# RWKV-7 preparation in a two-layer hybrid backbone: key norms inverted per token, products moved between engines, one tile of inverses per layer

## The chip, the cores and the metric

The kernel runs on one core of one Trainium2 chip. The metric is the device time of one execution in microseconds (us); lower is better. The core has a matrix engine (TensorE, PE in the tables; its weight loads are PEld), a vector engine (VectorE, DVE), a scalar engine (ScalarE, ACT), a general engine (GpSimd, POOL) and a queue that issues transfers (SyncE, SP). Each engine takes its instructions in a fixed order, and semaphores hold it where an input or a buffer is not yet ready.

## What is computed

The reference is a backbone of two layers over 256 latent and 256 context tokens of width 1024. In each layer one input projection feeds four token mixers (bidirectional RWKV-7, Hyena, a short gated convolution, grouped-query attention); their outputs are merged by sigmoid gates and projected, and a grouped top-2 mixture of 16 experts follows. The change concerns the RWKV mixer alone, of which this is the core:

```python
def rwkv_inputs(p, mu, w0, w_up, a0, a_up, k_k, k_a):
    ...
    kk = to_heads(k * k_k)
    kk = kk * lax.rsqrt(jnp.maximum(jnp.sum(kk * kk, -1, keepdims=True), 1e-24))
    k_dir = k[None] * (1.0 + (a - 1.0) * k_a)
    return to_heads(r), to_heads(k_dir), to_heads(v), kk, to_heads(a), to_heads(decay), gd

def wkv_scan(S0, r, decay, k, v, kk, a, reverse, emit):
    def step(S, inp):
        r_t, w_t, k_t, v_t, kk_t, a_t = inp
        S = (S * w_t[:, :, None, :]
             - jnp.einsum('bhvk,bhk->bhv', S, kk_t)[..., None] * (kk_t * a_t)[:, :, None, :]
             + v_t[..., :, None] * k_t[..., None, :])
        return S, (jnp.einsum('bhvk,bhk->bhv', S, r_t) if emit else None)
    ...
```

The four heads are 64 channels wide. A key is divided by its own norm, so only the product of the normalised key with itself times the rate a is needed (the kernel uses the square of the norm and one reciprocal). The state is carried from the context tokens to the latent tokens, in both directions; in layer 1 no context output is wanted, so the context stream there computes states only (emit is false).

## The kernel before

Channels lie on the 128 partitions (two heads each), tokens on the free axis. Per layer the program runs attention, then the RWKV input projections, then Hyena and the short convolution, then the RWKV core `recur()`, `merge()` with the gates, the output projection, a layer norm, the router and the experts. That is the order in which the code is written; a list scheduler in the framework sets, from this order as priority and a cost model of its own, one fixed sequence of instructions for each engine. So the many 128x512 projections (`mm3`, three products of split operands on L355 to L357, their weights split by ACT on L326 and by DVE on L327) and the modulation products (L394) stand between the RWKV instructions on PE and fill it there.

`recur()` makes four pairs per layer: stream s (0 context, 1 latent) by half b of the channels. Each pair is a generator `rwkv_pair` with four stages, and `recur()` interleaves them: stages 1 and 2 of the first pair; then, for each pair i, stage 1 of pair i+1, stage 3 of pair i, stage 2 of pair i+1, stage 4 of pair i.

- Stage 1, preparation, in tile R4. `kkr` = k times k_k (ACT, L872) and the squares in `at` (ACT, L873); PE adds the squares of a head with a matrix of ones, which leaves each sum on all 64 rows of its head (L876, 64x256); DVE takes the maximum with 1e-24 (L877), the reciprocal (L878) and the product with `kkr` (L879), giving `kkd`. Then for each direction d: two products on PE (L883, L884), two tanh on ACT (L885, L886, the second into `at` again), a running sum of the log decays on DVE (L889), two small offsets (L891, L892), exponentials on ACT (L894, L895), the directional key `kd` (ACT L896, POOL L898), and the four scaled operands: `ar` (DVE L904, POOL L906 if emit), `be` (DVE L908, L909) and `ka` (POOL L911), and three columns `sc` (L915 to L917). With emit, POOL L923 and DVE L924 prepare the bonus term.
- Stage 2, the triangular inverse. Products on PE (L936), masking on DVE (L938), the bonus on PE (L943, 128x2), a DVE copy (L944). The tile TZ takes the inverses of 16-token-group blocks: POOL clears it (L954, 128x2048) for each pair, DVE runs a serial loop of 15 steps (L968, L970, L976), ACT (L981, four instructions) and DVE (L982) write the result into TZ. TZ's buffer is single, so L954 waits for the last reader of the pair before, in its stage 4. In layer 0 the scratch of stage 2 is tile R4 too, the one of stage 1.
- Stage 3, the inverse level by level: PE L990, ACT L992, PE L998 and L1000, DVE L1003; then PE L1008, ACT L1010, and the second half of the tile (FZ) filled by DVE copies (L1012, L1013, 64x256), PE products and ACT copies (L1019, L1020).
- Stage 4, the recurrence over two groups of 128 tokens and both directions: PE L1039 to L1044 and DVE L1046; PE L1050 and ACT L1052 (`kb`); a scaled state Ss (DVE L1057); PE L1061 and L1064, ACT L1066 (Rs), PE L1070, DVE L1072 (Wn), and with Wn the state update on PE (L1079, L1080), a scaled state Sf (DVE L1077), the sum on DVE (L1099, L1101) and the outputs (PE L1084 to L1089, ACT L1092, DVE L1094).

After `recur()`, `finish()` normalises Y for `merge()`, which handles the branches in the order 2, 3, 1, 0; RWKV is branch 0.

## Time and profile before

| | us |
|---|---|
| median of 3 runs | 1911.12 |
| lowest and highest | 1905.01, 1916.12 |
| the profiled execution | 1914.72 |
| its span, first to last instruction | 1912.9 |
| mean granted clock of TensorE over the span | 0.934 |

| engine | busy, us | share of the span | instructions |
|---|---|---|---|
| PE | 1679.5 | 88% | 9683 |
| PEld | 1109.7 | 58% | 9683 |
| DVE | 884.5 | 46% | 1920 |
| ACT | 530.6 | 28% | 935 |
| POOL | 223.4 | 12% | 263 |

The durations below come from the profiled execution, whose time is 3.6 us above the median; 1.8 us of its time lie outside the span. Its RWKV cores lie at 270 to 510 us (layer 0) and 1250 to 1520 us (layer 1). [...]

### The profile page before, as it was taken

Reading aid. Unit: us, or ns where it says so; the run is one execution under the profiler, and the core shown is the slowest. Engines: PE = TensorE matmul, PEld = TensorE weight load, DVE = VectorE, ACT = ScalarE, POOL = GpSimd, SP = SyncE. Lnnn points to the kernel's source line nnn. Section 1 sums busy time; section 2 is a strip of 40 time slices with the busy share of each in tenths; the row PEclk is TensorE's granted clock in tenths of the full one; section 3 lists DMA queues with packets and bytes.
Section 4 is the critical chain, followed back from the end, with each engine's and each line's share of the span. In section 5 each row is a group of like instructions: output and inputs, shape, how many; then the busy total and the mean of one; then the engine's idle time right before and its main releaser. Section 6 shows DMA issues by size and latency. Waiting matters only on the chain. (4 is left out here: it accounts for less than half of the span.)

```text
span 1912.9 us, 24847 instructions
## 1 busy us (share of the span) xinstructions
PE 1679.5 (88%) x9683; PEld 1109.7 (58%) x9683; DVE 884.5 (46%) x1920; ACT 530.6 (28%) x935; POOL 223.4 (12%) x263
## 2 busy tenths in 40 slices
PE   4799999999999987999999919989889996999982
PEld 1467666766778875444444306767778895444430
DVE  4364458778554565101010076585887676200003
ACT  2253233433223311111011044543443352111101
POOL 4200121011000031000000041021120002000001
PEclk7899999999999995999999959988899997999996
DMA  9513553111243255883979953265212357879994
GB/s 367 212 40 131 183 188 111 50 62 51 76 138 116 101 196 191 287 337 117 378 273 375 403 196 129 82 224 192 67 62 86 117 180 289 337 281 420 420 421 163
DMA packets 123350, 384.82 MB, mean 201 GB/s; under 512 B 8791, under 2 KB 75103, under 8 KB 92383
## 3 DMA queue, kind: packets, MB, share of 16 engines
q1 hardware_dynamic: 106176, 329.41, 46.0%
q10 hardware_dynamic: 10238, 33.23, 4.7%
q0 software_dynamic: 6816, 20.58, 3.0%
q8 instruction: 77, 1.26, 0.3%
q14 instruction: 43, 0.34, 0.1%
HBM read 361.62 MB, written 21.56 MB: 200 GB/s over the span
## 5 line engine op out<-in xcount | busy, mean ns | idle before, releaser
L357 PE MATMUL acc<-hB,cv 128*128 128x512 f32 (+1 forms) x864 | 309.4, 359 | 9.9 <-POOL hB L616 9.8
L355 PE MATMUL acc<-hA,cv 128*128 128x512 f32 (+1 forms) x864 | 309.2, 358 | 7.1 <-ACT hA L610 3.9
L356 PE MATMUL acc<-hA,cv 128*128 128x512 f32 (+1 forms) x864 | 308.1, 357 | 4.2 <-DVE cv L327 4.2
L355 PEld LDWEIGHTS acc<-hA,cv 128*128 128x128 f32 x864 | 166.2, 192 | 44.6 <-issue 10.1
L357 PEld LDWEIGHTS acc<-hB,cv 128*128 128x128 f32 x864 | 165.8, 192 | 44.5 <-issue 12.8
L356 PEld LDWEIGHTS acc<-hA,cv 128*128 128x128 f32 x864 | 166.1, 192 | 34.4 <-issue 8.4
L327 DVE TENSOR_TENSOR cv<-ring,cv 128x1024 fp32r<-128x1024 f32 (+1 forms) x108 | 128.6, 1197 | 41.9 <-ACT cv L326 39.6
L1415 DVE TENSOR_TENSOR y<-XS,k 128x512 f32<-128x512 f32 x15 | 15.4, 1029 | 266.4 <-PE k L1403 265.7
L326 ACT ACTIVATE cv<-ring 128x1024 fp32r<-128x1024 f32 (+1 forms) x108 | 109.1, 1019 | 27.7 <-DMA ring<-in_w_in_dram 22.4
L1403 PE MATMUL k<-R,R 128*64 128x512 f32 (+1 forms) x288 | 108.5, 600 | 2.9 <-DMA R<-in_exp_w_dram 2.9
L394 PE MATMUL ada<-ring,csf 128*32 128x512 f32 x336 | 63.4, 665 | 13.3 <-ACT csf L230 10.1
L1403 PEld LDWEIGHTS k<-R,R 128*64 128x64 f32 (+1 forms) x288 | 36.6, 152 | 56.5 <-issue 50.8
L1323 ACT ACTIVATE gt<-acc 128x512 f32<-128x512 f32 (+1 forms) x64 | 31.3, 488 | 110.9 <-PE acc L357 102.7
L1403 PE MATMUL acc<-R,R 128*64 128x512 f32 (+1 forms) x160 | 60.3, 594 | 1.7 <-DMA R<-in_exp_w_dram 1.7
L1415 DVE TENSOR_TENSOR y<-XS,acc 128x512 f32<-128x512 f32 x7 | 7.2, 1028 | 114.4 <-PE acc L1403 114.4
L1332 DVE SCALAR_TENSOR_TENSOR gt<-gt,o 128x512 f32<-128x512 f32 (+1 forms) x48 | 26.5, 552 | 69.6 <-PE o L357 66.1
L1403 PE MATMUL k<-ring,R 128*64 128x512 f32 (+1 forms) x144 | 54.4, 609 | 0.0
L968 DVE TENSOR_TENSOR R<-R 128x32 f32<-128x32 f32 (+14 forms) x120 | 50.9, 424 | 1.7
L1535 DVE CAST m_ix<-o 128x1 int32<-128x1 f32 x14 | 2.2, 159 | 106.2 <-PE o L1533 106.2
L355 PE MATMUL o<-R,R 128*128 128x512 f32 (+1 forms) x128 | 45.7, 358 | 2.9 <-DVE R L1330 2.9
L357 PE MATMUL o<-R,R 128*128 128x512 f32 (+1 forms) x128 | 45.6, 358 | 1.1 <-DVE R L327 1.1
L1435 PE MATMUL k<-R,y 128*64 128x512 f32 (+1 forms) x124 | 45.6, 593 | 0.8 <-DVE y L1420 0.8
(565 smaller groups left out, 3386.7 us busy)
## 6 DMA issues: line engine op xcount, KB each, us to landing
R<-in_exp_w_dram SPq DMA_DIRECT2D x87, 1024.0 KB
ring<-in_w_in_dram SPq DMA_DIRECT2D x51, 1024.0 KB
ring<-in_ada_w_dram SPq DMA_DIRECT2D x42, 1024.0 KB
ring<-in_exp_w_dram SPq DMA_DIRECT2D x34, 1024.0 KB
cv<-in_exp_w_dram SPq DMA_DIRECT2D x31, 1024.0 KB
hB<-in_exp_w_dram SPq DMA_DIRECT2D x24, 1024.0 KB
TZ<-in_exp_w_dram SPq DMA_DIRECT2D x16, 1024.0 KB
y<-in_w_branch_dram SPq DMA_DIRECT2D x32, 256.0 KB
```

The costliest lines, as they stand in the source:

```text
L326: first = ACT.activation(hi, src, AF.Copy)
L327: DVE.tensor_tensor(lo, src, hi.bitcast(F32), op=OP.subtract)
L355: PE.matmul(o, lh, rh, start=start, stop=False)
L356: PE.matmul(o, ll, rh, start=False, stop=False)
L357: PE.matmul(o, lh, rl, start=False, stop=stop)
L394: PE.matmul(po[32 * q:32 * q + 32, :], csf[:, 2 * k:2 * k + 32], t[:, 512 * q:512 * q + 512], start=(k == 0), stop=(k == 7), skip_group_ch ...
L968: DVE.tensor_tensor(P4[:, :, :, :i + 1], T4[:, :, :, :i + 1], row[:, None, :, :].to_broadcast([128, 8, 2, i + 1]), op=OP.mult)
L1323: ACT.activation(gt, gp, AF.Tanh, scale=0.5)
L1332: DVE.scalar_tensor_tensor(gt, gt, 1.0, q, op0=OP.add, op1=OP.mult)
L1403: PE.matmul(q[c, :], t[:, k, c], w[x](k), start=(k == 0), stop=(k == 7), skip_group_check=n > 1)
L1415: DVE.tensor_tensor(t.rearrange("p (k c) -> p c k", k=4), act.rearrange("p (c k) -> p c k", k=4), p3.rearrange("p (c k) -> p c k", k=4), o ...
L1435: PE.matmul(p[h][c, :], t[:, k, c], w2[x](k)[:, h * 512:h * 512 + 512], start=(k == 0), stop=(k == 3), skip_group_check=n > 1)
```

## The change

It touches `recur()` and `rwkv_pair` in four ways.

- The key norms are inverted per token. The squares are now the stationary operand and `hones` (128x2, ones in the rows of one head per column) the moving one, so that PE leaves the four sums of a token on its own row (tokens on partitions, 128x4; new line L880). DVE takes maximum and reciprocal of the 128x4 tile `kkn` (L882, L883). ACT spreads the result, times -0.5, over 64 columns per head into `at` (L885), PE transposes the two 128x128 halves (L888), and DVE multiplies `kkr` with the product in PSUM (L889).
- The products on POOL (L898, L906, L911 and L923 of before: 16, 12, 16 and 6 instructions in a run) are DVE's (L908, L916, L921, L933).
- Four kinds of DVE instruction are ACT's: the FZ copies (L1012, L1013, 16 each), Ss (8), Wn (32) and Sf (16).
- The tile TZ is taken once per layer, in `recur()`, and cleared there as a whole. The pairs after the first clear the 1024 columns of the TZ half alone (new L964); FZ's zero blocks stay from the first clearing. The clearing now waits for the readers of the TZ half, in stage 3 of the pair before, and no more for those of FZ in its stage 4.

```diff
--- before.py
+++ after.py
@@ -798,8 +798,12 @@
         def recur():
             N8 = wt("y0", [128, 1024]).rearrange("p (m t) -> p m t", m=8)
             POOL.tensor_copy(N8, ident[:, None, :].to_broadcast([128, 8, 128]))
-
-            pairs = [rwkv_pair(l, s, b, ctx_out or s == 1, kT[b], rT[b], V, Y, wad, wa, bon, N8)
+            tz = unit("TZ")
+            TZ = tz[:, :1024].rearrange("p (m x t) -> p m x t", m=8, x=2)
+            FZ = tz[:, 1024:].rearrange("p (m t) -> p m t", m=8)
+            POOL.memset(tz, 0.0)
+
+            pairs = [rwkv_pair(l, s, b, ctx_out or s == 1, kT[b], rT[b], V, Y, wad, wa, bon, N8, TZ, FZ)
                      for s in range(2) for b in range(2)]
             next(pairs[0])
             next(pairs[0])
@@ -850,7 +854,7 @@
 
         return recur, finish
 
-    def rwkv_pair(l, s, b, emit, kTb, rTb, V, Y, wad, wa, bon, N8):
+    def rwkv_pair(l, s, b, emit, kTb, rTb, V, Y, wad, wa, bon, N8, TZ, FZ):
 
         ts_ = slice(256 * s, 256 * s + 256)
         k_, r_ = kTb[:, ts_], rTb[:, ts_]
@@ -872,11 +876,17 @@
         ACT.activation(kkr, k_, AF.Copy, scale=col("rwkv_k_k", l, b))
         ACT.activation(at, k_, AF.Square, scale=col("rwkv_k_k", l, b))
         q = rps()
-        for hp in heads:
-            PE.matmul(q[hp, :256], cc("ones")[hp, :64], at[hp, :], start=True, stop=True)
-        DVE.tensor_scalar(kkd, q[:, :256], 1e-24, None, op0=OP.max)
-        DVE.reciprocal(kkd, kkd)
-        DVE.scalar_tensor_tensor(kkd, kkd, -0.5, kkr, op0=OP.mult, op1=OP.mult)
+        for g in range(2):
+            PE.matmul(q[:, 2 * g:2 * g + 2], at[:, g * 128:g * 128 + 128], cc("hones"), start=True, stop=True)
+        n2 = wt("kkn", [128, 4])
+        DVE.tensor_scalar(n2, q[:, :4], 1e-24, None, op0=OP.max)
+        DVE.reciprocal(n2, n2)
+        n64 = at.rearrange("p (g h c) -> p (g h) c", g=2, h=2)
+        ACT.activation(n64, n2[:, :, None].to_broadcast([128, 4, 64]), AF.Copy, scale=-0.5)
+        q = rps()
+        for g in range(2):
+            PE.transpose(q[:, g * 128:g * 128 + 128], at[:, g * 128:g * 128 + 128], ident)
+        DVE.tensor_tensor(kkd, kkr, q[:, :256], op=OP.mult)
         AR, BE, KA, SC = [], [], [], []
         for d in range(2):
             q, qa = rps(), rps()
@@ -895,7 +905,7 @@
                 ACT.activation(en3[:, g], cu[:, g], AF.Exp, scale=0.5 * KAPPA, bias=mb[:, 1, g:g + 1])
             ACT.activation(kd[d], at, AF.Identity, scale=col("rwkv_k_a", l, b, pd),
                            bias=pf[:, l * 2 + b:l * 2 + b + 1])
-            POOL.tensor_tensor(kd[d], kd[d], k_, op=OP.mult)
+            DVE.tensor_tensor(kd[d], kd[d], k_, op=OP.mult)
             if d == 0:
                 inc, prev, inv = ep3[:, :, 1:], ep3[:, :, :128], en3[:, :, 1:]
             else:
@@ -903,12 +913,12 @@
             ar = E(512).rearrange("p (g x t) -> p g x t", g=2, x=2)
             DVE.tensor_tensor(ar[:, :, 0, :], g2(kkr), prev, op=OP.mult)
             if emit:
-                POOL.tensor_tensor(ar[:, :, 1, :], g2(r_), inc, op=OP.mult)
+                DVE.tensor_tensor(ar[:, :, 1, :], g2(r_), inc, op=OP.mult)
             be = E(256)
             DVE.scalar_tensor_tensor(be, at, 1.0, kkd, op0=OP.add, op1=OP.mult)
             DVE.tensor_tensor(g2(be), g2(be), inv, op=OP.mult)
             ka = E(256)
-            POOL.tensor_tensor(g2(ka), g2(kd[d]), inv, op=OP.mult)
+            DVE.tensor_tensor(g2(ka), g2(kd[d]), inv, op=OP.mult)
 
             sc = wt("ssc", [128, 3], bufs=4)
             e_in, e_out = (en3[:, :, 0:1], ep3[:, :, 128:129]) if d == 0 else (ep3[:, :, 128:129], en3[:, :, 0:1])
@@ -920,7 +930,7 @@
             KA.append(ka)
             SC.append(sc)
         if emit:
-            POOL.tensor_tensor(kd[0], kd[0], kd[1], op=OP.add)
+            DVE.tensor_tensor(kd[0], kd[0], kd[1], op=OP.add)
             DVE.scalar_tensor_tensor(kd[0], r_, col("rwkv_r_k", l, b), kd[0], op0=OP.mult, op1=OP.mult)
         yield
 
@@ -950,10 +960,8 @@
         ad = G_(256).rearrange("p (s u) -> p s u", u=8)
         TT_ = G_(256).rearrange("p (c j) -> p c j", c=8)
         o2 = G_(256).rearrange("p (c k u) -> p c k u", c=8, k=4)
-        tz = unit("TZ")
-        POOL.memset(tz, 0.0)
-        TZ = tz[:, :1024].rearrange("p (m x t) -> p m x t", m=8, x=2)
-        FZ = tz[:, 1024:].rearrange("p (m t) -> p m t", m=8)
+        if s or b:
+            POOL.memset(TZ.rearrange("p m x t -> p (m x t)"), 0.0)
         POOL.tensor_copy(TT_.rearrange("p c j -> p (c j)"), msk[:, 1024:1280])
         for x in range(4):
             xs_ = slice(32 * x, 32 * x + 32)
@@ -1009,8 +1017,8 @@
         xs = wt("XS", [128, 8, 64])
         ACT.activation(xs[lo_], q[lo_].rearrange("p (m t) -> p m t", m=8), AF.Copy)
         for hp in heads:
-            DVE.tensor_copy(FZ[hp, 0:4, hp], TZ[hp, 0:4, 1, :])
-            DVE.tensor_copy(FZ[hp, 4:8, hp], TZ[hp, 4:8, 0, :])
+            ACT.activation(FZ[hp, 0:4, hp], TZ[hp, 0:4, 1, :], AF.Copy)
+            ACT.activation(FZ[hp, 4:8, hp], TZ[hp, 4:8, 0, :], AF.Copy)
         q = rps()
         for m in range(4):
             PE.matmul(q[lo_, m * 64:m * 64 + 64], TZ[lo_, m, 0, :], xs[lo_, m, :], start=True, stop=True)
@@ -1054,7 +1062,7 @@
                 S = SBD[d, b]
                 if not first and step == 0:
                     Ss = wt("Ss", [128, 128], bufs=2)
-                    DVE.tensor_scalar(Ss, S, sc[:, 0:1], None, op0=OP.mult)
+                    ACT.activation(Ss, S, AF.Copy, scale=sc[:, 0:1])
                     S = Ss
                 q = rps()
                 for h in range(2):
@@ -1069,12 +1077,12 @@
                     hv = slice(h * 64, h * 64 + 64)
                     PE.matmul(q[:, hv], FZ[:, 4 * d + 2 * g + h, :], R[:, hv], start=True, stop=True)
                 W = wt("Wn", [128, 128], bufs=2)
-                DVE.tensor_copy(W, q[:, :128])
+                ACT.activation(W, q[:, :128], AF.Copy)
                 if update:
                     f = sc[:, 1 + step:2 + step]
                     if not first:
                         Sf = wt("Sf", [128, 128], bufs=2)
-                        DVE.tensor_scalar(Sf, S, f, None, op0=OP.mult)
+                        ACT.activation(Sf, S, AF.Copy, scale=f)
                     q = rps()
                     PE.matmul(q[:, :128], kb[:, 0, :], Vg, start=True, stop=False)
                     PE.matmul(q[:, :128], kb[:, 1, :], W, start=False, stop=True)
```

The sequences change as follows in three places. The names are tiles with their buffer numbers: k_ and acc_ are PSUM, R_ the working tiles, cst the constants (ones, `hones`, the identity), kkn_ the new 128x4 tile, cv_ and ring_ the weights of the projections.

PE, layer 0, preparation of the first pair, before:

```order
L357 MATMUL acc_1691<-hB_50_303,cv_229_1688 128x512
L876 MATMUL k_1727<-R_233_1724,cst 64x256 x2
L883 MATMUL k_1733<-R_146_866 128x256
L884 MATMUL k_1734<-R_146_866 128x256
L883 MATMUL k_1759<-R_146_866 128x256
L884 MATMUL k_1760<-R_146_866 128x256
```

and after:

```order
L357 MATMUL acc_1691<-hB_50_303,cv_229_1688 128x512
L880 MATMUL k_1729<-cst,R_234_1726 128x2 x2
L394 MATMUL ada_3359<-ring_3357,csf 32x512 x4
L355 MATMUL acc_3370<-hA_47_300,cv_513_3367 128x512
L356 MATMUL acc_3370<-hA_47_300,cv_513_3367 128x512
L357 MATMUL acc_3370<-hB_49_302,cv_513_3367 128x512
L355 MATMUL acc_3370<-hA_47_300,cv_513_3367 128x512
L356 MATMUL acc_3370<-hA_47_300,cv_513_3367 128x512
L888 MATMUL k_1736<-cst,R_234_1726 128x128 x2
L893 MATMUL k_1740<-R_146_866 128x256
L894 MATMUL k_1741<-R_146_866 128x256
```

Four modulation products and five projection products now stand between the norm's products and the transposes, and the products for the tanh (L893, L894) come behind the transposes.

PE, layer 1, preparation of the first pair, before:

```order
L356 MATMUL acc_7866<-hA_1140_6964,cv_1275_7863 128x256
L357 MATMUL acc_7866<-hB_1142_6966,cv_1275_7863 128x256
L876 MATMUL k_8340<-R_1324_8337,cst 64x256 x2
L883 MATMUL k_8346<-R_1243_7538 128x256
L884 MATMUL k_8347<-R_1243_7538 128x256
```

and after:

```order
L356 MATMUL acc_7883<-hA_1145_6981,cv_1280_7880 128x256
L357 MATMUL acc_7883<-hB_1147_6983,cv_1280_7880 128x256
L880 MATMUL k_8359<-cst,R_1330_8356 128x2 x2
L888 MATMUL k_8366<-cst,R_1330_8356 128x128 x2
L893 MATMUL k_8370<-R_1248_7555 128x256
L894 MATMUL k_8371<-R_1248_7555 128x256
```

Here the transposes stand directly behind the norm's products. In the other pairs of layer 1 there are about 100, 11 and 22 rows between the two; in the third and fourth of layer 0 there are five projection products, in the second three modulation and seven projection products.

ACT, layer 0, preparation of the second pair, before:

```order
L981 ACTIVATE TZ_1804<-R_246_1803 32x8x32 x4
L872 ACTIVATE R_249_1852<-R_144_864,pc 128x256
L873 ACTIVATE R_249_1852<-R_144_864,pc 128x256
L1323 ACTIVATE gt_3503<-acc_3478 128x512
L326 ACTIVATE cv_532_3562<-ring_3513 128x1024
L885 ACTIVATE R_249_1852<-k_1861,pd 128x256
L886 ACTIVATE R_249_1852<-k_1862,pd 128x256
```

and after:

```order
L1331 ACTIVATE gt_3520<-acc_3495 128x512
L876 ACTIVATE R_251_1857<-R_144_864,pc 128x256
L877 ACTIVATE R_251_1857<-R_144_864,pc 128x256
L326 ACTIVATE cv_537_3579<-ring_3530 128x1024
L326 ACTIVATE R_507_3350<-y_509_3354 128x512
L885 ACTIVATE R_251_1857<-kkn_1863 128x256
L895 ACTIVATE R_251_1857<-k_1871,pd 128x256
L896 ACTIVATE R_251_1857<-k_1872,pd 128x256
```

The spreading of the inverses (L885) stands behind two splits of weights (L326), and the tanh behind it.

## Rows read from the trace of the kernel before

**Rows 1.** Stretches: columns are us, busy (x) per engine, PEclk, DMA share, GB/s.
```profile
270.00:510.00 240.00, 221.45 (x1888) 163.69 (x1886) 187.49 (x451) 92.06 (x182) 37.41 (x41) 0.96 0.23 80
510.00:700.00 190.00, 189.15 (x857) 152.50 (x857) 94.86 (x157) 55.91 (x77) 16.94 (x12) 1.00 0.34 111
1250.00:1520.00 270.00, 245.71 (x2308) 206.51 (x2306) 204.75 (x501) 109.33 (x216) 43.14 (x47) 0.92 0.34 112
310.00:320.00 10.00, 6.85 (x46) 4.06 (x47) 6.42 (x13) 6.91 (x14) 0.72 (x1) 0.67 0.00 0
```

**Rows 2.** Waits of PE, 250 to 550 us: total, times, longest.
```profile
PE k L990 <- DVE TZ L1003: 6.3, 4, 2.7
PE k L876 <- ACT R L873: 5.2, 3, 3.4
PE k L936 <- DVE R L909: 2.0, 1, 2.0
...
PE k L883 <- DVE R L877: 1.0, 1, 1.0
```

**Rows 3.** Waits of PE, 1230 to 1640 us.
```profile
PE k L990 <- DVE TZ L982: 6.3, 5, 2.4
...
PE acc L356 <- DVE cv L327: 3.7, 2, 2.8
PE o L355 <- DVE R L1330: 2.9, 2, 1.9
PE o L1135 <- DVE R L1132: 2.2, 1, 2.2
```

**Rows 4.** Timeline of PE, layer 0: start, us, instruction, idle before.
```profile
271.09 0.65 PE L876 MATMUL k<-R,cst 64*64 64x256 f32 x4
...
287.05 0.58 PE L943 MATMUL k<-cst,R 128*128 128x2 f32 x4 [0.44 <-DVE R L924]
...
313.15 0.91 PE L876 MATMUL k<-R,cst 64*64 64x256 f32 x4 [3.35 <-ACT R L873]
```

**Rows 5.** One line of PE: ns min/median/max, first and last start.
```profile
L1050 PE MATMUL k<-cst,R x24: 271/273/273, 340.4 to 1491.2; 128*128 128x128 f32 x24
```

**Rows 6.** Groups of DVE by form: busy, mean ns | idle before, releaser.
```profile
L878 DVE RECIPROCAL R<-R 128x256 f32<-128x256 f32 x8 | 14.0, 1747 | 0.1
...
L1072 DVE COPY Wn<-k 128x128 f32<-128x128 f32 x32 | 9.3, 290 | 20.7 <-PE k L1070 20.6
...
L1012 DVE COPY TZ<-TZ 64x256 f32<-64x256 f32 x16 | 4.6, 285 | 0.3
L879 DVE SCALAR_TENSOR_TENSOR R<-R 128x256 f32<-128x256 f32 x8 | 4.3, 537 | 0.0
L1269 DVE RECIPROCAL amx<-amx 128x1 f32<-128x1 f32 x24 | 3.9, 162 | 4.4 <-ACT R L1268 3.7
L877 DVE TENSOR_SCALAR R<-k 128x256 f32<-128x256 f32 x8 | 3.3, 416 | 4.1 <-PE k L876 2.5 <-ACT gt L1323 1.5
```

**Rows 7.** One line of DVE: ns min/median/max, first and last start.
```profile
L904 DVE TENSOR_TENSOR R<-R x16: 408/874/958, 279.9 to 1428.1; 128x256 f32<-128x256 f32 x16
```

**Rows 8.** Groups of POOL by form.
```profile
L954 POOL MEMSET TZ<- 128x2048 f32 x8 | 14.5, 1809 | 145.4 <-PE k L1070 60.9 <-DVE R L970 29.7 <-ACT Rs L1066 29.6
L898 POOL TENSOR_TENSOR R<-R,R 128x256 f32<-128x256 f32 x16 | 14.2, 889 | 91.6 <-ACT R L896 87.1 <-issue 4.6
```

**Rows 9.** Groups of ACT by form.
```profile
L326 ACT ACTIVATE cv<-ring 128x1024 fp32r<-128x1024 f32 x100 | 104.4, 1051 | 27.7 <-DMA ring<-in_w_in_dram 22.4 <-DMA ring<-in_w_out_dram 2.8 <-PE acc L357 2.3
...
L1066 ACT ACTIVATE Rs<-k 128x128 f32<-128x128 f32 x32 | 8.8, 275 | 41.8 <-PE k L1064 36.4 <-PE k L1061 5.1
...
L885 ACT ACTIVATE R<-k,pd 128x256 f32<-128x256 f32 x16 | 7.6, 472 | 10.7 <-DVE cu L889 7.7 <-PE k L884 2.8
```

**Rows 10.** Waits of ACT, 250 to 550 us.
```profile
ACT TZ L981 <- POOL TZ L954: 6.4, 3, 2.7
```

## The prediction

> **What bounds the kernel now.** I read the stretches first. From 510 to 700 us PE is busy 189.15 of 190 us at clock 1.00, so nothing is to be had there. In the two RWKV stretches it is not full [rows 1]: idle are 240 − 221.45 = 18.6 us in layer 0 and 270 − 245.71 = 24.3 us in layer 1, 42.9 us together. [...] The clock falls where PE is thinly fed: from 310 to 320 us, where it is idle 3.15 of 10 us, the row has 0.67. DVE is next, with 187.49 and 204.75 us busy; ACT and POOL are far below. So PE sets the time. Outside its own work, the change can give back only PE's waits and the clock that goes with them. DVE, ACT and POOL count only through the instructions that PE waits for.
>
> Second, PE's waits. In layer 0 the large ones are 6.3 us for DVE L1003, 5.2 for ACT L873, 2.0 for DVE L909 and 1.0 for DVE L877 [rows 2]; in layer 1, 6.3 for DVE L982, 3.7 for L327, 2.9 for L1330 and 2.2 for L1132 [rows 3]. Nearly all name DVE; the one that names ACT does so because ACT began the squares only after stage 2 of the pair before (the tile R4 is shared), which ends on DVE's loop. The wait for L1003 is different: PE, ACT and DVE hand one level of the inverse to each other and none is late by its queue alone.
>
> **The change part by part.** *PE's own work.* Removed are the norm's products, two per pair that stand as four in the trace, 0.65 us: 8 × 0.65 = 5.2 us. Added are two 128x2 products and two transposes per pair [rows 4, 5]. The nearest row to the former is L943, the same shape, count and type, 0.58 us; a transpose moves 128 columns like L1050, 0.27 us, 0.55 the two. 8 × (0.58 + 0.55) = 9.0 us; net **+3.8 us**, on the path.
>
> *DVE's ledger.* Removed are L877 to L879 (3.3 + 14.0 + 4.3 = 21.6 us), Wn (9.3), the FZ copies (L1012 with 4.6 and its twin L1013, 9.2), and Ss and Sf, 24 instructions of Wn's shape at 0.29 = 7.0: 47.1 us [rows 6]. Added are 50 products. L904 is the same shape and takes from 408 ns to 958, with a median of 874 [rows 7]; the low end is what it costs with POOL quiet, which is how it will be, so 50 × 0.41 = 20.5 us. The rest of the norm adds 0.16 twice (the 128x1 reciprocal, L1269) and 0.42 (L877's 128x256 from PSUM): 8 × 0.74 = 5.9 us [rows 6]. POOL's absence also shortens what stays: L904's sixteen come from 12.4 us (16 × 0.772) to 6.5, and L909 as many of the same shape, an estimate of 11.8 us for both. DVE ends 47.1 + 11.8 − 26.4 = 32.5 us lighter of 392 in the two stretches [rows 1, 6, 7]. Of the 20.6 us in which DVE stood at Wn for PE, work behind Wn in its queue is freed too; part comes back one instruction later, at the state's sum (L1099), and I give it no sum of its own.
>
> The row of the reciprocal is 1747 ns for 256 columns and 162 for one [rows 6], which makes the narrow norm worth 8 × 1.59 = 12.7 us of DVE. [...]
>
> *ACT.* It gains 32 Wn and 24 Ss and Sf at L1066's 0.275 (15.4 us), 32 FZ copies between 0.275 and 0.472 (about 12) and 8 spreads at 0.47 (3.8): 31 us on 201 in the stretches [rows 1, 9]. It has room, so its load costs nothing; its order can, below. *POOL* loses 50 × 0.89 = 44 us and half of its clearings [rows 8], all beside PE.
>
> *Waits that go.* The 8.2 us of layer 0 behind L873, L909 and L877 and the 15.1 us of layer 1 are 23.3 us [rows 2, 3]. The preparation's DVE work gets shorter by about 2 us in each norm and 0.45 in each L904 and L909. The clearing of TZ no longer waits for stage 4, where ACT stood 6.4 us for it [rows 10], which brings stage 2 forward. But PE also arrives earlier by what it has gained, so a later wait on the same chain is partly there again. I take two thirds: **−15.5 us**; bounds 0 and −23.3. The 6.3 us at L1003 stay.
>
> *Clock.* Where the idle time goes the clock should come nearer to 1.00. Two thirds of 23.3 us are about a third of the 42.9 us idle; I take a quarter of 31.2 because the smaller gaps of the inverse remain: **−7.8 us**; bounds 0 and −15.6.
>
> *The new wait.* Between the norm's products and the transposes lies a round trip: DVE 0.16 + 0.16 and ACT 0.47 make 0.8 us [rows 6, 9]; with the handovers, for which no row stands, I take 1.0. PE's order puts five to seven projection products there in layer 0, at 189.15 / 857 = 0.22 us each [rows 1], 1.1 us and more, and nothing at the first pair of layer 1. So one place pays 1.0 us in any case (the second pair of layer 1 has about 100 products and pays nothing). At the six others the cover is just the bare round trip: with one split of weights ahead of the spread in ACT's queue (L326, 1.05 us [rows 9]) PE stands that long, and everything behind the transposes on PE stands with it. 6 × 1.05 + 1.0 = **+7 us**; bounds +1 and, at the longest wait that the trace has at this place (3.35 us [rows 4]), 8 × 3.35 = +27.
>
> Sum: +3.8 − 15.5 − 7.8 + 7 = −12.5 us. The profiled execution goes from 1914.7 to 1902.2; against the median of 1911.1, which the forecast is about, 1898.6. The difference of 3.6 us between the two is neither gain nor loss.
>
> **The rivals.** *Greater gain, 1879.* All 23.3 us of waits go, half of the clock's 31.2 comes back, and the transposes cost 3 us: +3.8 − 23.3 − 15.6 + 3 = −32.1. For it: nearly every wait names DVE, and DVE loses a twelfth of its load. Against: the chain of the inverse stays serial.
>
> *No change, 1910.* PE's order is planned with the same shorter chain, so the stages stand as close as before and the waits come back a little earlier in the program. A quarter of 23.3 goes (−6), the clock gives 2, PE's work costs 3.8 and the transposes half of 7: −0.7. For it: the 18.6 and 24.3 us of idle time are spread over many small gaps, and the largest single waits are at the levels of the inverse, which the change leaves alone. [...]
>
> *Slower, 1926.* PE's order is static and ACT's too. The spread of the inverses stands in ACT's queue behind splits of 1.05 us and copies of whole projections, and the transposes hold all of PE until it is done; later, Rs and Wn, both now ACT's, stand behind the four writes of TZ. If the eight places cost 3.35 us each and, with these pauses, the clock gives nothing back: +3.8 − 15.5 + 26.8 = +15.1. It decides from 8h = 9.6 + 15.5 − 3.8, so h = 2.7 us per place. For it: in the layer-0 order, two splits stand directly ahead of the spread of the second pair, and in layer 1 the first pair has no cover. Against: 2.7 us would need two or three such instructions at every place.
>
> **How the numbers follow.** The measurement of this kernel can tell about 0.5%, 9.6 us, from no change: faster is below 1901.6, slower above 1920.7. Forecast (1889 to 1904, around 1898.6) 0.41; greater gain 0.15; no change 0.27; slower 0.17. The forecast's upper edge lies in the band of no change, so some of it (0.07) counts there: faster 0.49, same 0.34, slower 0.17. The range runs from 1878, just past the greater gain's sum, to 1920, where it takes in all of no change; beyond are a little under half of the greater gain (0.06) and most of the slower case (0.13).
>
> **What would show it.** Right: the stretch of layer 0 shorter by about 4 us and that of layer 1 by about 8, clocks near 0.97 and 0.94; L904's successor near 0.41 us; no wait of PE for the squares above 2 us; a wait at the transposes for ACT of about 1 us a place; DVE about 32 us lighter. Wrong: a wait at the transposes of 2 us or more a place (slower); the waits for L1003 and L982 as large as before or larger, and the clocks unchanged (no change); a moved product on DVE that still takes 0.8 us, which would say that POOL was not what stretched L904; or a gap of PE outside the two stretches, in `merge()` or the experts, that the moved transfers open.

## The result and the profile after

The changed kernel takes 1894.1 us (median of 7 runs, 1892.8 to 1904.3); the kernel before, beside it, 1916.0 (7 runs, 1905.0 to 1921.5). The ratio is 0.9899, with a 95% interval of 0.9871 to 0.9927: 1.0% faster, 19 us by the ratio. The forecast, 1898.6 us or a gain of 12.5, had the sign and about two thirds of the size. What carried it, the experiments show, was a part that the prediction had booked as a loss. One execution of the kernel with the products alone, further below, took 2848.5 us at a clock of 0.548 and is left out of its ratio, which rests on the three others.

The table of busy times of the changed kernel, to be set beside the one of before:

```profile
PE 1671.1 (88%) x9699; PEld 1105.2 (58%) x9699; DVE 850.0 (45%) x1882; ACT 563.2 (30%) x1031; POOL 176.6 (9%) x213
```

DVE is 34.5 us lighter and ACT 32.6 us heavier; the ledger said 32.5 and 31. The stretches of [rows 1], after (PEclk, the last column but two, is the granted clock, 1.00 being full speed):

```profile
270.00:510.00 240.00, 227.55 (x1958) 170.69 (x1951) 172.26 (x446) 108.56 (x233) 12.43 (x13) 0.99 0.24 81
510.00:700.00 190.00, 187.33 (x832) 151.23 (x830) 98.33 (x159) 57.17 (x78) 20.42 (x15) 1.00 0.36 123
1250.00:1520.00 270.00, 251.07 (x2463) 216.49 (x2462) 197.47 (x479) 133.06 (x270) 21.24 (x25) 0.98 0.38 126
```

Both RWKV stretches hold more PE work in the same time (1958 matmul records for 1888, 2463 for 2308) at clocks of 0.99 and 0.98, for 0.96 and 0.92. To compare equal work I cut each trace at the same instructions: layer 0 from the first L1157 (Hyena) to the first product of the router, L1859; layer 1 from the last L1280 (attention) to where the last group of L1859 begins (line numbers of the kernel before). Before:

```profile
224.64:706.46 481.82, 461.98 (x2977) 353.67 (x2977) 301.98 (x634) 155.32 (x268) 64.60 (x66) 0.98 0.30 101
1214.61:1612.65 398.04, 357.90 (x3058) 305.83 (x3055) 287.97 (x617) 162.20 (x297) 54.97 (x56) 0.93 0.44 151
```

and after:

```profile
222.92:696.29 473.37, 459.23 (x2986) 353.52 (x2986) 282.94 (x618) 171.39 (x316) 39.52 (x38) 0.99 0.30 103
1205.55:1587.00 381.45, 346.73 (x3066) 297.80 (x3063) 271.32 (x595) 178.77 (x345) 33.07 (x34) 0.97 0.45 158
```

Layer 0 is 8.4 us shorter, layer 1 16.6. Idle time of PE (span less busy) falls from 19.8 to 14.1 and from 40.1 to 34.7 us, 11.1 together; busy time falls by 2.7 and 11.2, 13.9 together, although PE has more to do, as the clock is nearer to 1.00 (0.98 to 0.99 and 0.93 to 0.97 in the rows). The two cuts give 25.0 us and the span of the run 20.7. The rest comes back in the parts that the change doesn't touch: between the cuts (508.1 to 509.3 us) and after the second (264.8 to 268.0 to PE's last instruction). Over all kernels below these vary from 507.7 to 512.0 and from 263.7 to 268.2 us, so nothing follows from them.

PE's waits in layer 0, after, for [rows 2]:

```profile
PE k L880 <- ACT R L877: 4.3, 2, 3.2
PE k L998 <- DVE TZ L1011: 2.9, 3, 2.0
PE k L1078 <- ACT Rs L1074: 2.5, 4, 1.0
```

and in layer 1 (1210 to 1640 us), for [rows 3]:

```profile
...
PE acc L355 <- ACT cv L326: 2.8, 6, 1.1
PE acc L356 <- DVE cv L327: 2.6, 3, 1.2
PE k L1078 <- ACT Rs L1074: 2.4, 3, 1.2
PE o L1143 <- DVE R L1140: 2.0, 1, 2.0
PE k L946 <- DVE R L919: 1.6, 1, 1.6
PE k L998 <- DVE TZ L1011: 1.6, 2, 1.3
PE k L998 <- POOL R L965: 1.3, 1, 1.3
...
PE k L998 <- DVE TZ L990: 1.2, 3, 0.9
...
PE k L888 <- ACT R L885: 1.0, 1, 1.0
```

L998 is the old L990 and L1011 the old L1003. The wait for the squares hardly moved (5.2 to 4.3, the longest 3.2, where the prediction wanted none above 2). At the levels of the inverse, the wait for L1003, which the prediction left standing, went from 6.3 to 2.9 in layer 0. In layer 1 the wait for the writes of stage 2 went from 6.3 to 1.2, but the same product L998 now also waits 1.6 for L1011 and 1.3 for POOL's L965. Together that is 4.1 us, for 7.4 at L990 before (6.3 for L982, 0.3 for L1003, 0.8 for nothing that the profile shows). The two rows left out at the top of the list, 12.2 for L1861 and 3.8 for L1507, lie behind the RWKV core and are the same before (L1853, L1499). The new wait at the transposes (L888) is 1.0 us at one place in layer 1, the one without cover, and no other place is in these lists.

Groups of DVE by form, after (busy, mean ns | idle before):

```profile
L914 DVE TENSOR_TENSOR R<-R 128x256 f32<-128x256 f32 x16 | 7.6, 472 | 0.5
L921 DVE TENSOR_TENSOR R<-R 128x256 f32<-128x256 f32 x16 | 6.7, 417 | 0.0
...
L889 DVE TENSOR_TENSOR R<-R,k 128x256 f32<-128x256 f32 x8 | 3.4, 419 | 10.6 <-PE k L888 10.5
...
L883 DVE RECIPROCAL kkn<-kkn 128x4 f32<-128x4 f32 x8 | 1.4, 170 | 0.1
```

L914 is the old L904, whose median was 874 ns [rows 7]; its mean is now 472, its median 420, with one at 1255. A product moved from POOL (L921) takes 0.42 us, for 0.96 there (L911 of before, 15.3 us for 16). The narrow reciprocal takes 0.17 us for the 1.75 of the wide one.

### The profile page after: what moved, and what is told of

It reads as the page before. It is cut to its first block, busy times and chain, and to the rows that moved or that the text cites. A ratio compares the mean times of both kernels' runs of the same rounds, so it can differ in the third digit from the quotient of the medians.

```text
span 1892.2 us, 24863 instructions
## 1 busy us (share of the span) xinstructions
PE 1671.1 (88%) x9699; PEld 1105.2 (58%) x9699; DVE 850.0 (45%) x1882; ACT 563.2 (30%) x1031; POOL 176.6 (9%) x213
## 5 line engine op out<-in xcount | busy, mean ns | idle before, releaser
L327 DVE TENSOR_TENSOR cv<-ring,cv 128x1024 fp32r<-128x1024 f32 (+1 forms) x108 | 127.1, 1183 | 34.5 <-ACT cv L326 34.2
L326 ACT ACTIVATE cv<-ring 128x1024 fp32r<-128x1024 f32 (+1 forms) x108 | 109.0, 1019 | 18.5 <-DMA ring<-in_w_in_dram 11.6
L355 PE MATMUL o<-R,R 128*128 128x512 f32 (+1 forms) x128 | 44.7, 349 | 0.6 <-DVE gt L1340 0.6
L1559 ACT ACTIVATE R<-o 128x512 f32<-128x512 f32 x28 | 16.4, 597 | 96.7 <-PE o L1558 96.7
```

The costliest lines, as they stand in the source:

```text
L326: first = ACT.activation(hi, src, AF.Copy)
L327: DVE.tensor_tensor(lo, src, hi.bitcast(F32), op=OP.subtract)
L355: PE.matmul(o, lh, rh, start=start, stop=False)
```

## The experiments

Three theories stood at the start. **A**: PE waits for DVE's queue, and what makes DVE lighter (norm, copies) gives the time; this is the prediction's. **B**: TZ, taken once per layer, lets stage 2 begin earlier. **C**: no part counts; each edit makes the scheduler write another sequence, and some are better.

### One part undone

The changed kernel with the wide norm of before:

```diff
-        for g in range(2):
-            PE.matmul(q[:, 2 * g:2 * g + 2], at[:, g * 128:g * 128 + 128], cc("hones"), start=True, stop=True)
...
-        DVE.tensor_tensor(kkd, kkr, q[:, :256], op=OP.mult)
+        for hp in heads:
+            PE.matmul(q[hp, :256], cc("ones")[hp, :64], at[hp, :], start=True, stop=True)
+        DVE.tensor_scalar(kkd, q[:, :256], 1e-24, None, op0=OP.max)
+        DVE.reciprocal(kkd, kkd)
+        DVE.scalar_tensor_tensor(kkd, kkd, -0.5, kkr, op0=OP.mult, op1=OP.mult)
```

> The changed kernel with the wide norm of before (128x256 reciprocal on DVE, no transposes). Theory A (PE waits because DVE's queue is late; what lightens DVE's preparation gives time): DVE gets 21.6 - 5.9 = 16 us heavier in the two stretches, PE's own work 3.8 us lighter; half of the gain of 20 us goes, time about 8 us above the changed kernel (ratio to before about 0.994). Theory B (TZ taken once per layer lets stage 2 begin earlier, and that is the gain): within 4 us of the changed kernel. Theory C (the gain is one of the fixed sequences that the scheduler happens to write, not of any part): moves by up to 8 us either way, unrelated to DVE's load.

Measured: ratio to before 0.9917 (0.9892 to 0.9942). The interval holds the changed kernel's 0.9899, and theory A's 0.994 as well, so this run decides nothing.

The products back on POOL:

```diff
-            DVE.tensor_tensor(kd[d], kd[d], k_, op=OP.mult)
+            POOL.tensor_tensor(kd[d], kd[d], k_, op=OP.mult)
...
-                DVE.tensor_tensor(ar[:, :, 1, :], g2(r_), inc, op=OP.mult)
+                POOL.tensor_tensor(ar[:, :, 1, :], g2(r_), inc, op=OP.mult)
...
-            DVE.tensor_tensor(g2(ka), g2(kd[d]), inv, op=OP.mult)
+            POOL.tensor_tensor(g2(ka), g2(kd[d]), inv, op=OP.mult)
...
-            DVE.tensor_tensor(kd[0], kd[0], kd[1], op=OP.add)
+            POOL.tensor_tensor(kd[0], kd[0], kd[1], op=OP.add)
```

> The changed kernel with the 50 products back on POOL. Theory A: DVE gets 20.5 us lighter by the products and about 12 us heavier by the contention (DVE's L914 back from 0.47 to about 0.8 us); net 8 lighter, but the products wait on POOL 0.9 us each in the chain of the preparation; time 0 to 4 us above the changed kernel. Theory B: within 4 us. Theory C: up to 8 us either way.

Measured: 1.0038 (1.0018 to 1.0058), slower than before. With everything else of the change in place, the whole gain is gone. That is some 26 us above the changed kernel, where A had at most 4 and C at most 8: no theory foresaw it. Its table of busy times:

```profile
PE 1683.9 (88%) x9699; PEld 1118.9 (58%) x9699; DVE 852.9 (44%) x1832; ACT 563.3 (29%) x1031; POOL 216.1 (11%) x263
```

DVE is 31.6 us lighter than before, as light as in the changed kernel within 3 us, and the kernel is slower than before. So DVE's sum is not what sets the time, and theory A falls as a price by that sum; that PE waits for DVE's queue is left open by it. Its largest wait of PE in layer 0:

```profile
PE k L998 <- DVE TZ L1011: 12.4, 4, 4.1
```

The wait at the levels of the inverse is twice that of before.

The copies back on DVE:

```diff
-            ACT.activation(FZ[hp, 0:4, hp], TZ[hp, 0:4, 1, :], AF.Copy)
-            ACT.activation(FZ[hp, 4:8, hp], TZ[hp, 4:8, 0, :], AF.Copy)
+            DVE.tensor_copy(FZ[hp, 0:4, hp], TZ[hp, 0:4, 1, :])
+            DVE.tensor_copy(FZ[hp, 4:8, hp], TZ[hp, 4:8, 0, :])
...
-                    ACT.activation(Ss, S, AF.Copy, scale=sc[:, 0:1])
+                    DVE.tensor_scalar(Ss, S, sc[:, 0:1], None, op0=OP.mult)
...
-                ACT.activation(W, q[:, :128], AF.Copy)
+                DVE.tensor_copy(W, q[:, :128])
...
-                        ACT.activation(Sf, S, AF.Copy, scale=f)
+                        DVE.tensor_scalar(Sf, S, f, None, op0=OP.mult)
```

> The changed kernel with FZ, Ss, Wn and Sf back on DVE. Theory A: DVE 25 us heavier and again standing at Wn for PE (20.6 us of such idle time before), with the preparation of the next pair behind it; about 8 us above the changed kernel. Theory B: within 4 us. Theory C: up to 8 us either way.

Measured: 0.9886 (0.9843 to 0.9930), the same as the changed kernel.

TZ taken and cleared for each pair:

```diff
...
-        if s or b:
-            POOL.memset(TZ.rearrange("p m x t -> p (m x t)"), 0.0)
+        tz = unit("TZ")
+        POOL.memset(tz, 0.0)
+        TZ = tz[:, :1024].rearrange("p (m x t) -> p m x t", m=8, x=2)
+        FZ = tz[:, 1024:].rearrange("p (m t) -> p m t", m=8)
```

(and without the taking and clearing in `recur()`)

> The changed kernel with TZ taken and cleared for each pair, so that stage 2 of a pair waits again for the stage 4 of the pair before. Theory A: ACT stands for the clearing again (6.4 us in layer 0 before), PE waits for TZ 2 to 4 us more; about 3 us above the changed kernel. Theory B: most of the gain goes, 12 us or more above the changed kernel. Theory C: up to 8 us either way.

Measured: 0.9887 (0.9840 to 0.9935), the same as the changed kernel. Theory B falls.

### One part alone

These are the same edits the other way, on the kernel of before.

```diff
...
-        DVE.tensor_scalar(kkd, q[:, :256], 1e-24, None, op0=OP.max)
-        DVE.reciprocal(kkd, kkd)
...
+        DVE.tensor_scalar(n2, q[:, :4], 1e-24, None, op0=OP.max)
+        DVE.reciprocal(n2, n2)
...
```

> The kernel of before with the narrow norm alone. Theory A: DVE 16 us lighter, PE's own work 3.8 us more; about 6 us faster than before (0.997). Theory B (the single TZ is the gain): within 4 us of before. Theory C (an accident of the scheduler's sequences): up to 8 us either way.

Measured: 1.0015 (0.9992 to 1.0038), no change.

```diff
-            POOL.tensor_tensor(kd[d], kd[d], k_, op=OP.mult)
+            DVE.tensor_tensor(kd[d], kd[d], k_, op=OP.mult)
...
```

(and so for the other three lines)

> The kernel of before with the 50 POOL products on DVE alone. Theory A: DVE 20.5 us heavier by the products, 12 us lighter by the contention, so 8 us heavier: between the same and 4 us slower than before. Theory B: within 4 us. Theory C: up to 8 us either way.

Measured: 0.9890 (0.9824 to 0.9956): the move of the products alone is worth as much as the whole change. This too lies outside all three theories; A had it the same to 4 us slower. Its table of busy times:

```profile
PE 1669.4 (88%) x9683; PEld 1104.2 (58%) x9683; DVE 876.6 (46%) x1970; ACT 530.2 (28%) x935; POOL 180.4 (10%) x213
```

DVE has 50 instructions more than before and is 7.9 us less busy.

```diff
-                DVE.tensor_copy(W, q[:, :128])
+                ACT.activation(W, q[:, :128], AF.Copy)
...
```

(with FZ, Ss and Sf)

> The kernel of before with FZ, Ss, Wn and Sf on ACT alone. Theory A: DVE 25 us lighter and no longer held at Wn; about 8 us faster than before (0.996). Theory B: within 4 us. Theory C: up to 8 us either way.

Measured: 1.0045 (1.0023 to 1.0068), slower. Why was not settled; beside the products' move the copies do no harm that can be measured.

```diff
+            tz = unit("TZ")
...
+            POOL.memset(tz, 0.0)
...
-        tz = unit("TZ")
-        POOL.memset(tz, 0.0)
...
+        if s or b:
+            POOL.memset(TZ.rearrange("p m x t -> p (m x t)"), 0.0)
...
```

> The kernel of before with TZ taken once per layer alone. Theory A: 2 to 3 us faster than before. Theory B: 12 us or more faster. Theory C: up to 8 us either way.

Measured: 1.0014 (0.9989 to 1.0039), no change.

The eight kernels and the two given ones divide by one thing. The cut of layer 0 takes 467.1 to 473.5 us where the products are on DVE (five kernels) and 481.8 to 493.1 where they are on POOL (five); the cut of layer 1 takes 381.5 to 389.5 and 391.1 to 403.0. Each is of one execution. That leaves three ways: **D**, POOL's products slow DVE's instructions beside them; **E**, the products' own time and hand-over on POOL counted, or the sequence that the scheduler writes for them (what is left of C).

### The same sequence, with and without POOL beside it

A kernel with the products on DVE and two small buffers single, which frees the room for a spare tile:

```diff
-                    Ss = wt("Ss", [128, 128], bufs=2)
+                    Ss = wt("Ss", [128, 128])
...
-                        Sf = wt("Sf", [128, 128], bufs=2)
+                        Sf = wt("Sf", [128, 128])
```

> The kernel of before with the 50 products on DVE, and the buffers Ss and Sf single (this frees 1 KB a partition, which the next kernel needs; it changes 734 of 5669 rows of PE's order). The control for the next one. All theories: within 6 us of the products on DVE alone (ratio to before 0.989), so 0.986 to 0.992; further off would show how much the order alone is worth.

Measured: 0.9915 (0.9889 to 0.9940). 734 rows of PE's sequence differ from the products on DVE alone, and the cut of layer 0 takes 467.25 us for 467.06, that of layer 1 392.14 for 389.54 (the expectation of the last run below has 390.8, from a cut that ended 1.3 us later). So another sequence moved the cuts by 0.2 and 2.6 us, where the products' move had taken 14.8 and 8.5 us off them. That is one other sequence: it speaks against C, and the next run decides.

To that, as many products on POOL, into a tile that nobody reads:

```diff
+            jk = wt("junk", [128, 256])
+            POOL.tensor_tensor(g2(jk), ar[:, :, 0, :], g2(k_), op=OP.mult)
+            if emit:
+                POOL.tensor_tensor(g2(jk), ar[:, :, 0, :], g2(r_), op=OP.mult)
             be = E(256)
...
+            POOL.tensor_tensor(jk, be, k_, op=OP.mult)
...
+            POOL.tensor_tensor(jk, ka, r_, op=OP.mult)
```

> The same kernel, with 50 products of the same size done on POOL besides, into a spare tile that nobody reads (extra work; the result is untouched). PE's and ACT's orders are the same row for row as in the control. Theory D (POOL's products slow DVE's instructions beside them, and this is what the move removed): DVE's L904 and its neighbours are back at 0.7 to 0.9 us, and as there are now 82 such products on DVE, the time is at least as long as before: 15 us or more above the control. Theory E (what counted was the products' own time and hand-over on POOL, or the order that the scheduler writes for it): within 4 us of the control.

Measured: 1.0043 (1.0026 to 1.0059); medians 1923.9 against the control's 1898.2 us, 25.7 us more, from work that no instruction waits for, under the same sequence of PE and ACT; DVE's 1970 instructions, too, come in the same order in the two traces. ACT is as busy in the cuts of the one as of the other (318.1 and 318.0 us), and its wait for the clearing of TZ on POOL doesn't grow (8.2 and 8.0 us in layer 0). So D is shown, and it is large enough for the whole gain; E isn't needed, but that the hand-over on POOL cost nothing at all is not shown. The two cuts of the control:

```profile
224.60:691.85 467.25, 456.35 (x2977) 349.62 (x2977) 297.29 (x662) 155.34 (x268) 43.30 (x38) 1.00 0.31 104
1200.12:1592.26 392.14, 353.13 (x3059) 301.66 (x3055) 285.72 (x639) 162.75 (x297) 33.89 (x34) 0.95 0.45 154
```

and with POOL's spare products:

```profile
222.32:706.04 483.72, 464.07 (x2977) 354.69 (x2977) 309.75 (x662) 155.19 (x268) 69.77 (x66) 0.98 0.30 101
1218.04:1619.57 401.53, 357.95 (x3059) 305.27 (x3055) 293.09 (x639) 162.81 (x297) 52.26 (x56) 0.93 0.44 150
```

The cuts lengthen by 16.5 and 9.4 us, which is all of it. PE does the same matmuls in both; idle it is 13.3 us longer (10.9 to 19.7 and 39.0 to 43.6), busy 12.5 us longer, at the lower clock (by an estimate from these rows, 456.35 us at 1.00 would be 465.7 at 0.98; it is 464.07). DVE is 19.8 us longer busy for the same 1301 records.

Most of the idle time is at the levels of the inverse. PE's wait there in layer 0, control and spare products:

```profile
PE k L990 <- DVE TZ L1003: 2.6, 3, 2.1
```

```profile
PE k L996 <- DVE TZ L1009: 9.3, 5, 2.9
```

In layer 1 its waits for the two writers of TZ on DVE go from 6.0 to 8.8 us, so the two layers have 9.5 of the 13.3 us.

Where it lands is seen in layer 0, in the preparation of the third pair, beside which the inverse of the second goes on. The timeline of DVE in the control, from the last products of a preparation to the next level of the inverse:

```profile
374.19 0.40 DVE L904 TENSOR_TENSOR R<-R 128x256 f32<-128x256 f32 x1
...
375.59 0.14 DVE L916 TENSOR_TENSOR ssc<-R 128x1 f32<-128x1 f32 x1
...
375.86 0.41 DVE L898 TENSOR_TENSOR R<-R,R 128x256 f32<-128x256 f32 x1
376.19 0.41 DVE L908 SCALAR_TENSOR_TENSOR R<-R 128x256 f32<-128x256 f32 x1
...
377.95 0.42 DVE L911 TENSOR_TENSOR R<-R 128x256 f32<-128x256 f32 x1
...
378.82 0.73 DVE L1003 COPY_PREDICATED TZ<-msk,k 128x512 f32<-128x512 uint8 x1
```

and with POOL busy beside it, the same instructions:

```profile
380.56 0.41 DVE L904 TENSOR_TENSOR R<-R 128x256 f32<-128x256 f32 x1
...
381.96 0.64 DVE L921 TENSOR_TENSOR ssc<-R 128x1 f32<-128x1 f32 x1
...
382.72 0.98 DVE L898 TENSOR_TENSOR R<-R,R 128x256 f32<-128x256 f32 x1
383.62 0.97 DVE L912 SCALAR_TENSOR_TENSOR R<-R 128x256 f32<-128x256 f32 x1
...
385.92 0.96 DVE L915 TENSOR_TENSOR R<-R 128x256 f32<-128x256 f32 x1
...
387.81 0.71 DVE L1009 COPY_PREDICATED TZ<-msk,k 128x512 f32<-128x512 uint8 x1
```

Beside the first three of the slowed instructions POOL has these:

```profile
381.11 1.47 POOL L908 TENSOR_TENSOR junk<-R,R 128x256 f32<-128x256 f32 x1 [11.79 <-DVE R L904]
382.66 0.76 POOL L910 TENSOR_TENSOR junk<-R,R 128x256 f32<-128x256 f32 x1
383.50 0.81 POOL L916 TENSOR_TENSOR junk<-R,R 128x256 f32<-128x256 f32 x1
```

From L904's start to the end of the masked copy it is 5.36 us and 7.96 us. The copy itself takes no longer; it stands behind products that do. PE, in the second:

```profile
388.58 0.89 PE L996 MATMUL k<-TZ,y 64*64 64x64 f32 x16 [2.40 <-DVE TZ L1009]
```

It stood 2.40 us for that copy, and in the control not at all. It is the kind of wait that [rows 2] have as 6.3 us for L1003.

Groups of DVE by form, the control:

```profile
L911 DVE TENSOR_TENSOR R<-R 128x256 f32<-128x256 f32 x16 | 6.9, 428 | 0.0
...
L916 DVE TENSOR_TENSOR ssc<-R 128x1 f32<-128x1 f32 x16 | 2.3, 147 | 0.0
...
L915 DVE COPY ssc<-R 128x1 f32<-128x1 f32 x16 | 2.3, 141 | 0.0
```

and with the spare products:

```profile
L915 DVE TENSOR_TENSOR R<-R 128x256 f32<-128x256 f32 x16 | 11.3, 709 | 0.0
...
L921 DVE TENSOR_TENSOR ssc<-R 128x1 f32<-128x1 f32 x16 | 9.0, 560 | 0.0
...
L904 DVE TENSOR_TENSOR R<-R 128x256 f32<-128x256 f32 x16 | 7.7, 479 | 0.0
...
L920 DVE COPY ssc<-R 128x1 f32<-128x1 f32 x16 | 2.2, 140 | 0.0
```

Instructions with two operands in SBUF are slowed, even one of a single column (0.147 to 0.560 us); the copy of a single column beside it (L920, the control's copy at L915), with one, is not, although 10 of the 16 overlap a product on POOL. The wide reciprocal has one operand too. No spare product lies beside it here, but in the kernel before L898 on POOL overlaps six of its eight, and all eight take 1741 to 1753 ns:

```profile
431.72 1.75 DVE L878 RECIPROCAL R<-R 128x256 f32<-128x256 f32 x1
```

```profile
432.33 0.73 POOL L898 TENSOR_TENSOR R<-R,R 128x256 f32<-128x256 f32 x1 [1.43 <-ACT R L896]
```

One sign of D failed: L904 was to be back at 0.7 to 0.9 us and takes 0.479 in the mean. The first spare product waits for L904 itself, so POOL is mostly quiet while it runs; those behind it are hit.

### Part of the products, and the best of both

32 of the 50 products on DVE:

```diff
-            POOL.tensor_tensor(kd[d], kd[d], k_, op=OP.mult)
+            DVE.tensor_tensor(kd[d], kd[d], k_, op=OP.mult)
...
-            POOL.tensor_tensor(g2(ka), g2(kd[d]), inv, op=OP.mult)
+            DVE.tensor_tensor(g2(ka), g2(kd[d]), inv, op=OP.mult)
```

> The kernel of before with 32 of the 50 products (kd times k, L898, and ka, L911) on DVE, the other 18 (r's operand, L906, and the sum of kd, L923) left on POOL. Theory D: the contention goes in proportion, 32/50 of the gain of about 20 us, 13 us: ratio 0.993, and L904 at about 0.55 us. Theory E: all of the gain or none of it, as these two products are the ones that matter or not.

Measured: 0.9939 (0.9917 to 0.9962), 0.6% for the 1.1% of all 50, and L904 takes 0.506 us in the mean: about in proportion, as D has it. All of the gain is not excluded, as the interval overlaps that of the 50 (0.9824 to 0.9956). By the cuts it is half of the gain in layer 0 (474.0 us, between 467.1 and 481.8), where 12 of 28 products were left on POOL, and all of it in layer 1 (389.1 beside 389.5), where 6 of 22 were.

The products on DVE in both layers, the other three parts in layer 1 alone:

```diff
-            DVE.tensor_copy(FZ[hp, 0:4, hp], TZ[hp, 0:4, 1, :])
-            DVE.tensor_copy(FZ[hp, 4:8, hp], TZ[hp, 4:8, 0, :])
+            if l:
+                ACT.activation(FZ[hp, 0:4, hp], TZ[hp, 0:4, 1, :], AF.Copy)
+                ACT.activation(FZ[hp, 4:8, hp], TZ[hp, 4:8, 0, :], AF.Copy)
+            else:
+                DVE.tensor_copy(FZ[hp, 0:4, hp], TZ[hp, 0:4, 1, :])
+                DVE.tensor_copy(FZ[hp, 4:8, hp], TZ[hp, 4:8, 0, :])
...
```

(and the norm, Ss, Sf, Wn and TZ in the same way)

> The 50 products on DVE in both layers, the rest of the change (norm, copies, one TZ) in layer 1 alone: layer 0 has the order of the kernel with the products alone row for row, layer 1 nearly that of the changed kernel. From the stretches of the profiles (layer 0: 467.1 us with the products alone, 473.4 with everything; layer 1: 390.8 and 381.5): about 6 us faster than the changed kernel, ratio to before 0.986 to 0.987. If the differences of 6 and 9 us between the stretches are only how one execution differs from another: the same as the changed kernel, 0.990.

Measured: 0.9862 (0.9836 to 0.9888), 1889.0 us in the median of 6. It is the fastest of all; its interval overlaps that of the changed kernel (0.9871 to 0.9927), so the 0.4% between them are not secured. The cuts repeat the pattern: layer 0 takes 469.1 us for the changed kernel's 473.4; in layer 1, where the other three parts are in, 384.4 and 381.5 us stand against 389.5 and 392.1 with the products alone. So the other parts look worth some 5 to 11 us in layer 1, and seem to cost a few in layer 0. Which of them has it can't be told: layer 1 takes 389.4 us without the norm, 387.2 without the copies on ACT and 385.1 without the single TZ, and these three losses add up to more than the gain. Each of these cuts is of one execution.

## Why the prediction came out as it did

- **What bounds the kernel**: right. All of the gain lies in the two RWKV cuts, on PE's idle time and its clock.
- **DVE's ledger**: the step that failed. It booked 20.5 us for the 50 products and 11.8 us back from the contention, so 8.7 us on the wrong side, and the only part of the change to which it gave a loss on DVE is the one that made the gain. Only L904 and L909 had been counted. What the control gives back is 884.5 + 21.0 (its 50 products) − 877.7 = 27.8 us, more than the products cost: L904 5.8, L909 5.2, the 128x1 product L916 3.5 (360 to 147 ns), the scans L889 2.3, the weights' splits L327 about 3, and smaller groups. The trace of before had it: L904's line has a minimum of 408 ns and a median of 874 [rows 7], and its neighbours on DVE could have been read in the same way (L916 has 143, 227 and 693 as minimum, median and maximum). And a sum of DVE's time was the wrong measure even where it is right: without the products' move DVE was 31.6 us lighter and the kernel slower.
- **The products' move**: alone it gives 0.9890. The two engines slow each other (DVE's L898 from 0.41 to 0.98 us beside the spare products; POOL's first one, beside two-operand products of DVE, takes 1.47 us for the 0.76 and 0.81 of the next ones), and so the products cost less in one queue. What is slowed, the groups above show: L916, with two operands in SBUF, goes from 0.147 to 0.560 us, while the copy beside it, with one, has 0.141 and 0.140.
- **"None is late by its queue alone"**, of the 6.3 us at L1003: wrong. DVE's copy there stood behind the preparation's products, as the timelines above show for one place, and the wait fell to 2.9 us with the change, to 2.6 in the control, and rose to 9.3 with the spare products.
- **Norm and copies**, which carried most of the −15.5 us: alone 1.0015 and 1.0045, neither faster. The 12.7 us of DVE that the reciprocal gave are real (14.0 to 1.4 us), but they bought no time that these runs can tell from none; with the products moved, the norm, copies and TZ together may be worth 5 to 11 us in layer 1. The copies also have a price on ACT: PE's waits for Rs rose from 1.9 to 4.9 us (2.5 in layer 0, 0.3 there with the copies back on DVE).
- **Waits, net of the new one**: forecast −15.5 + 7 = −8.5, measured −11.1 of idle time. The mix is another: of the 23.3 us of waits that were booked, the lists after still have 11.4, so 11.9 went and not 15.5 (of the 5.2 for the squares only 0.9), while 3.4 came from L1003, booked at nothing. The new wait was oversized: 1.0 us at the one uncovered place, as said for it, and none of the six others with the 1.05 us each.
- **PE's own work**: +3.8 forecast; the lines take 7.6 us (4.2 at L880, 3.4 at L888) for 5.5 at L876, so +2.2.
- **Clock**: undersized. Busy time fell by 13.9 us in spite of the added work, where −7.8 + 3.8 = −4.0 was forecast; layer 1 went from 0.93 to 0.97 in its cut. That a full clock would give back 31.2 us, of which a quarter was booked, no run shows: it was the author's estimate, 0.04 × 240 + 0.08 × 270 us from the clocks of [rows 1] against 1.00. What the runs showed is 0.99 and 0.98 for 0.96 and 0.92 in these stretches, and the 13.9 us. So the sum of −12.5 us, for about −19, came as near as it did because misses cancelled: norm, copies and the new wait were set too high, the products and the clock too low. That it had the right sign was in part luck.
- **Slower**: its mechanism, PE held at the transposes, did not occur.

## What to carry to other kernels

Two engines that slow each other are not priced by moving work from one to the other at the uncontended duration: look in the trace for the spread between minimum and mean of every instruction that runs beside the work to be moved, and add all of it up. Here that spread was worth more than the moved work cost (27.8 us against 21.0). An engine's total is no measure of what it costs: here DVE at 852.9 us made a slower kernel than DVE at 876.6. What counted here is how late the one instruction came for which PE stood, and that is read by listing what is ahead of it in its queue.

## What the runs showed of the hardware

- POOL's products of two SBUF operands stretch the instructions of DVE with two SBUF operands that run beside them, from 0.41 to as much as 0.98 us (128x256) and from 0.15 to 0.56 us in the mean (128x1). A DVE copy or reciprocal with one operand in SBUF keeps its time beside POOL's products (0.14 us beside the spare ones, 1.75 us in the kernel before). The time added to the small product, 0.50 us in the row above, is nearly that of the large one, 0.55. The slowed rows end 0.02 to 0.28 us after POOL's product beside them, and POOL's own first product, which began at 381.11 us while DVE was still busy with two-operand products of its own (to 381.97), takes 1.47 us where the next ones take 0.76 and 0.81. By these rows it looks like a wait of each engine for the other's instruction and not like a slower rate; that is the author's estimate from them, and no run tested it.
- Products that nobody waits for cost 25.7 us of a 1898 us kernel, on an engine that is 12% busy. About half of it is PE's idle time and about half its longer busy time at the lower clock: in layer 0 the granted clock of the cut is 1.00 without them and 0.98 with them, in layer 1 0.95 and 0.93.
